# Retention's projections by Strassen's seven products for all heads first, results kept in DRAM, then the heads one by one

## The chip, the cores and the metric

The kernel runs on one core of one Trainium2 chip. Its time is device microseconds of that core; the figure of a kernel is the median of its runs. TensorE (PE in the profile) multiplies matrices into PSUM; VectorE (DVE) and ScalarE (ACT) work elementwise; GpSimd (POOL) works elementwise more slowly and issues DMAs, among them those that add into their target; SyncE (SP) issues the other DMAs.

## The reference

A decoder trunk of two layers on 512 tokens of 1024 features, in fp32. Each layer: half a SwiGLU FFN (2816 wide), a token mixer, half a FFN, a gated per-layer embedding. The mixer of layer 0 is retention with four heads, which is what the change touches:

```python
q, k, v, g = jnp.split(h @ w_in, ...)      # per head: 256, 256, 512, 512 columns
q = rotary(q, pos); k = rotary(k, pos) * DK ** -0.5
s = (q @ k.T) * decay                      # causal, per head
o = rmsnorm(s @ v, gn_w)                   # in chunks with a carried state; the kernel does it in one
y = silu(g) * o
h = h + y @ w_out
```

## The kernel before

Everything is kept transposed, features on partitions and the 512 tokens along the row. An fp32 value is split into a high part (a rounding to fp32r, made on ACT) and a low part (value minus high, DVE); a product is three matmuls, high x high, high x low, low x high (`mm3`, L330 to L332; `v_part` for values, L727 to L729; `product`, L515, for Strassen's). TensorE's instructions run in the order in which the code writes them; the other engines' order is made by a planner that places instructions as their inputs and tiles come free.

`Weights` holds a plan: the order in which weight tiles of 128 x 1024 are taken. `take` loads two tiles ahead (SP's queue), splits the tile on ACT and `W.low` (L85, L86; `W.low` is DVE, in the retention POOL) and has three buffers, `w8`. A `Pair` is Strassen's unit: two blocks of 128 output columns by two halves of the input features. Its two diagonal quarters get high and low parts in a `w8` tile: by ACT and DVE if the pair is marked `direct`, else by `negated` (L131 to L133): high on ACT, minus the raw value on ACT, then a DMA from POOL that adds the raw value into it. Four sums of quarters are made and split (`emit_sums_now`, L165), up to two pairs ahead. The FFNs take most pairs so: `start`, `one`, `two` begin pair m + 1 (three products) before `three` ends pair m (four products), with merges of PSUM banks between (L569 to L589); a pair is seven products of 12 matmuls of 256 columns. For this the norm makes seven forms of the activations per pair of feature blocks (`Norm.quarters`), where a plain projection needs only the high and low parts (`Norm.halves`).

The retention (L737 on) goes head by head, in plain projections `proj`, 24 matmuls of 512 columns for a block of 128 output columns: two query and two key blocks, `rotate`, the values (96 matmuls), the scores of the four key blocks with their decay and split (L819, `uhi`, `ulo`), then the previous head's output blocks or gate blocks, the products of scores and values (48 matmuls), gates, the scale of the head (`head_scale`, L773; `on_rows` with four transposes, L481, and a copy, L781) and the four outputs on DVE (L865, L869, L321). The output projections of the last two heads are summed in PSUM (`OutBoth`), and each finished block of h goes through the next norm's `quarters`.

The forgetting layer's values take weights by the adding DMA too (L133, `w<-in_fox_v`).

## Time and profile before

| what | value |
|---|---|
| median of three runs (lowest, highest) | 2148.61 us (2147.91, 2148.78) |
| profiled execution: time, span | 2147.82 us, 2145.9 us |
| TensorE busy, of the span | 2121.2 us, 99% |
| DVE, ACT, POOL busy | 1465.0, 1207.4, 355.9 us |
| retention, 348.6 to 752.6 us | 404.0 us |
| DVE, ACT, POOL busy in it | 183.2, 158.1, 143.4 us |
| granted TensorE clock | 0.998 |

How to read it: a TensorE that is busy throughout says only that matmuls follow each other; how long a stage takes is read from the number and width of its matmuls and the time between them. A row of a window gives its length, then busy time and number of instructions for each engine, the granted clock, the mean share in which the core's 16 DMA engines are busy, and GB/s. A row of a group ends in busy time, mean duration in ns, and the idle time just before with what ended it.

### The profile page before, as it was taken

The page shows a single profiled execution, that of the slowest core. Times are in us where ns is not written, and L with a number is a line of the kernel's source. Part 1 is how long each engine was busy: PE and PEld are TensorE (multiplying, and loading weights), DVE is VectorE, ACT ScalarE, POOL GpSimd, SP SyncE. Part 2 cuts the span into 40 slices and gives each one's busy share as a digit, 9 for nine tenths or more (in the row PEclk, how much of TensorE's full clock was granted, in tenths as well). Part 3 has the DMA queues.
Part 4 walks back from the last instruction along what each step waited for, and adds up shares of the span by engine and source line. Part 5 has one row for each costly group of instructions (what it writes and reads, how often), then busy time and mean ns, then how long its engine had stood idle before and what let it go on. Part 6 is the DMA issues. An engine that isn't in the chain of part 4 may idle for free.

```text
span 2145.9 us, 34373 instructions
## 1 busy us (share of the span) xinstructions
PE 2121.2 (99%) x13537; PEld 1917.5 (89%) x13537; DVE 1465.0 (68%) x2682; ACT 1207.4 (56%) x2036; POOL 355.9 (17%) x275
## 2 busy tenths in 40 slices
PE   9999999999999999999999999999999999999998
PEld 9899998888888898989989999998788799999987
DVE  8786876262533687868768787776675687877775
ACT  8474653333333664736557565555786775655655
POOL 0010100344444110201001011010234200100100
PEclk9999999999999999999999999999999999999999
DMA  6475652222222244746426466564522234655631
GB/s 192 119 177 134 161 150 93 88 94 79 89 79 89 91 124 131 181 124 174 130 94 153 125 169 155 142 148 122 144 84 93 80 99 125 171 153 142 158 108 40
DMA packets 92642, 268.39 MB, mean 125 GB/s; under 512 B 9392, under 2 KB 12976, under 8 KB 92480
## 3 DMA queue, kind: packets, MB, share of 16 engines
q1 hardware_dynamic: 63328, 209.78, 29.6%
q0 software_dynamic: 27920, 55.32, 15.7%
q8 instruction: 106, 1.74, 0.3%
q10 hardware_dynamic: 1232, 1.09, 0.2%
q14 instruction: 56, 0.46, 0.1%
HBM read 264.02 MB, written 2.13 MB: 124 GB/s over the span
## 4 chain that ended last, share of the span: by engine, by line
PE 84%; DVE 7%; ACT 5%; DMA 2%; issue 1%; SPq 0%; ACTq 0%; DVEq 0%
PE bank L515 35%; PE bank L330 13%; PE bank L332 13%; PE bank L331 13%; PE bank L550 3%; PE bank L728 2%; PE bank L727 2%; PE bank L729 2%; ACT p L1037 1%; DVE w L86 1%; DMA wraw<-in_ffn_w_in 1%; ACT p L1039 1%; DVE tlo L321 1%; ACT w L85 1%; DVE acc L454 1%
## 5 line engine op out<-in xcount | busy, mean ns | idle before, releaser
L85 ACT CAST w<-wraw 128x1024 fp32r<-128x1024 f32 (+1 forms) x234 | 238.5, 1022 | 420.1 <-PE bank L332 256.6
L330 PE MATMUL bank<-unit_a,w 128*128 128x512 f32 x736 | 287.9, 391 | 0.3 <-DVE tmp L1071 0.3
L331 PE MATMUL bank<-unit_a,w 128*128 128x512 f32 x736 | 286.6, 389 | 0.8 <-DVE unit_a L321 0.8
L332 PE MATMUL bank<-unit_a,w 128*128 128x512 f32 x736 | 286.6, 389 | 0.7 <-DVE w L86 0.7
L85 ACT CAST s<-sums 128x512 fp32r<-128x512 f32 x316 | 185.4, 618 | 149.7 <-PE bank L515 74.6
L330 PE MATMUL bank<-unit_d,w 128*128 128x512 f32 (+1 forms) x712 | 267.6, 376 | 1.0 <-DVE unit_b L324 0.6
L331 PE MATMUL bank<-unit_d,w 128*128 128x512 f32 (+1 forms) x712 | 266.8, 375 | 0.7 <-DVE unit_d L321 0.7
L332 PE MATMUL bank<-unit_d,w 128*128 128x512 f32 (+1 forms) x712 | 266.6, 374 | 0.0
L86 DVE TENSOR_TENSOR s<-sums,s 128x512 fp32r<-128x512 f32 x316 | 208.6, 686 | 60.9 <-ACT s L85 60.1
L86 POOL TENSOR_TENSOR w<-wraw,w 128x1024 fp32r<-128x1024 f32 x74 | 177.2, 2396 | 298.2 <-ACT w L85 293.3
L86 DVE TENSOR_TENSOR w<-wraw,w 128x1024 fp32r<-128x1024 f32 (+1 forms) x160 | 186.4, 1166 | 25.8 <-ACT w L85 25.7
L515 PE MATMUL bank<-unit_b,s 128*128 128x256 f32 x872 | 183.1, 276 | 0.0
L515 PE MATMUL bank<-unit_d,s 128*128 128x256 f32 x1140 | 178.3, 276 | 0.0
L133 POOL DMA_DIRECT2D a<-in_ffn_w_in x80 | 70.7, 884 | 630.0 <-ACT a L132 481.3
L515 PE MATMUL bank<-unit_a,s 128*128 128x256 f32 x1224 | 170.0, 276 | 0.0
L613 DVE SCALAR_TENSOR_TENSOR tmp<-bank,rows 128x512 f32<-128x512 f32 x96 | 66.2, 690 | 150.0 <-PE bank L332 149.9
L332 PEld LDWEIGHTS bank<-unit_a,w 128*128 128x128 f32 x736 | 138.2, 188 | 29.9 <-DVE w L86 1.1
L330 PEld LDWEIGHTS bank<-unit_a,w 128*128 128x128 f32 x736 | 138.2, 188 | 29.3 <-DVE tmp L1071 0.5
L331 PEld LDWEIGHTS bank<-unit_a,w 128*128 128x128 f32 x736 | 138.2, 188 | 29.2 <-DVE unit_a L321 1.2
L330 PEld LDWEIGHTS bank<-unit_d,w 128*128 128x128 f32 x712 | 133.8, 188 | 25.6 <-PE bank L1008 0.9
L331 PEld LDWEIGHTS bank<-unit_d,w 128*128 128x128 f32 x712 | 133.8, 188 | 24.4 <-DVE unit_d L321 1.0
L332 PEld LDWEIGHTS bank<-unit_d,w 128*128 128x128 f32 x712 | 133.7, 188 | 24.1
(295 smaller groups left out, 4758.7 us busy)
## 6 DMA issues: line engine op xcount, KB each, us to landing
wraw<-in_ffn_w_in SPq DMA_DIRECT2D x174, 512.0 KB, 4.4
wraw<-in_ffn_w_out SPq DMA_DIRECT2D x64, 512.0 KB, 4.4
w<-in_ffn_w_in POOLq DMA_DIRECT2D x57, 512.0 KB, 5.7
a<-in_ffn_w_in POOLq DMA_DIRECT2D x79, 256.0 KB, 6.2
wraw<-in_ffn_w_out SPq DMA_DIRECT2D x32, 384.0 KB, 3.7
wraw<-in_ret_qk SPq DMA_DIRECT2D x16, 512.0 KB, 3.5
wraw<-in_ret_v SPq DMA_DIRECT2D x16, 512.0 KB, 3.6
wraw<-in_ret_g SPq DMA_DIRECT2D x16, 512.0 KB, 3.5
```

The lines of the kernel that those rows point to most:

```text
L85: self.nc.scalar.copy(hi, raw)
L86: self.low.tensor_tensor(out=lo, in0=raw, in1=hi.bitcast(F32), op=ALU.subtract)
L133: self.nc.gpsimd.dma_start(out=lo, in_=src, accum_op=ALU.add)
L330: nc.tensor.matmul(out, wh, xh, start=first, stop=False)
L331: nc.tensor.matmul(out, wh, xl, start=False, stop=False)
L332: nc.tensor.matmul(out, wl, xh, start=False, stop=last)
L515: add = lambda w, x, start, stop: nc.tensor.matmul(out, w, x, start=start, stop=stop, skip_group_check=True)
L550: nc.tensor.matmul(o[:, HALVES[t]], x[:, ks], y, start=k == t == q == 0, stop=k == KB - 1 and q == 2, skip_group_check=True,)
L613: nc.vector.scalar_tensor_tensor(out=t1, in0=o, scalar=-0.5, in1=n.r, op0=ALU.mult, op1=ALU.mult)
L727: nc.tensor.matmul(os[t], xh, wh[:, js], start=k == 0, stop=False)
L728: nc.tensor.matmul(os[t], xh, wl[:, js], start=False, stop=False)
L729: nc.tensor.matmul(os[t], xl, wh[:, js], start=False, stop=k == KB - 1)
```

## The change

Strassen's pair code moves from the FFN into a class with `begin`, `rest` and `join` that hold the same operations. All four heads' queries and keys (eight pairs) and the gates of heads 1 to 3 (six pairs) are computed by it, so the norm ahead of the retention now makes the seven forms (with the corner `b12` in the tiles `ud`). The stage's order on TensorE is: values of head 1; pairs q1, k1; values of head 2; q2, k2, q3; values of head 3; k3, q0, k0; values of head 0; the six gate pairs. A pair's first three products stand ahead of the last four of the pair before it, across a values stage too. Rotated queries and keys of heads 1 to 3, all values and the gates of heads 1 to 3 (after SiLU) are written to DRAM by POOL's DMAs, 256 KB each; head 0's queries and keys stay on the chip, and its gates are computed later by plain products. The pairs 0 and 1 are `direct`, the others are not.

Then the heads run one by one. Each loads its queries, keys, values and gates from DRAM (SP's queue) and splits them again; scores and products follow each other, heads 1 to 3 with nothing between; output blocks of earlier heads stand elsewhere. The products loop over key blocks first, so that a head's four banks end together, and the sum of squares is on DVE, no longer on POOL. `W.low` stays DVE throughout; the output weights of heads 0 and 1 come by the adding DMA. Tile pools `ua` and `ud` change places in the FFNs behind. The weights' layout on the host follows.

```diff
+RET_V = {1: 2, 4: 3, 7: 0}
...
+    ret_order = [(x, hd) for hd in (1, 2, 3, 0) for x in "qk"] + [(x, hd) for hd in (1, 2, 3) for x in "01"]
...
-    ret_qk = [[a["ret_qk"][c] for c in (2 * h, 2 * h + 1, 8 + 2 * h, 9 + 2 * h)] for h in range(RH)]
     ret_v = [[a["ret_v"][h][:, c * 1024 : (c + 1) * 1024] for c in range(4)] for h in range(RH)]
-    ret_g = [[a["ret_g"][4 * h + c] for c in range(4)] for h in range(RH)]
+    ret_g = [[a["ret_g"][c] for c in range(4)]]
+    at = {"q": 0, "k": 4, "0": 8, "1": 9}
+    ret_pairs = []
+    for kind, hd in ret_order:
+        i = at[kind] + (hd if kind in "qk" else 2 * (hd - 1))
+        ret_pairs.append(Pair(4, a["ret_p"][i, 0], a["ret_p"][i, 1]))
+    ret_pairs[0].direct = ret_pairs[1].direct = True
...
     plan_ffn(0)
-    for h in range(RH - 1):
-        W.plan += ret_qk[h] + ret_v[h]
-        if h > 0:
-            W.plan += ret_o[h - 1]
-        W.plan += ret_g[h]
-    W.plan += ret_qk[RH - 1] + ret_v[RH - 1] + ret_g[RH - 1][0:2] + ret_o[RH - 2][0:1] + ret_g[RH - 1][2:4]
-    W.plan += ret_o[RH - 2][1:2]
+    W.plan += ret_v[1] + ret_pairs[0:1]
+    for i in range(len(ret_pairs)):
+        W.plan += ret_pairs[i + 1 : i + 2]
+        if i in RET_V:
+            W.plan += ret_v[RET_V[i]]
+    W.plan += ret_g[0] + ret_o[0] + ret_o[1] + ret_o[2][0:2]
     W.plan += [ret_o[i][c] for i, c in ((RH - 1, 0), (RH - 2, 2), (RH - 1, 1), (RH - 1, 2), (RH - 2, 3), (RH - 1, 3))]
...
+    def proj_forms(src, n):
+
+        wh, wl = W.take(src)
+        o = bank()
+        for t, half in enumerate(HALVES):
+            for k in range(KB):
+                ks = slice(k * P, (k + 1) * P)
+                xh, xl = n.forms[k // 2][f"b{1 + k % 2}{1 + t}"]
+                for q, (w, x) in enumerate(((wh, xh), (wh, xl), (wl, xh))):
+                    nc.tensor.matmul(
+                        o[:, half], w[:, ks], x, start=k == t == q == 0, stop=k == KB - 1 and q == 2,
+                        skip_group_check=True,
+                    )
+        return [o]
+
...
+    class Strassen:
+
+
+        def __init__(self, n):
+            self.n, self.live = n, {}
+
...
+        def rest(self, pair):
+            c0, c1 = HALVES
+            forms = self.n.forms
+            g, u, cc = self.live[id(pair)]
+            product(u[:, c0], pair.t[1], 0, forms, "t4")
+            product(g[:, c1], pair.s[3], 0, forms, "b22")
+            product(u[:, c1], pair.s[2], 0, forms, "t3")
+            product(g[:, c0], pair.x, 0, forms, "b21")
+
+        def join(self, pair):
...
+            return g, u
+
...
                     mm3(o, wh[:, js], wl[:, js], *act[k], k == k0, k == k1 - 1)
             for m, o in zip(ms, os):
+                if m == KB - 1 and c == len(chunks) - 1 and nxt.early and nxt.extra:
+                    nxt.corner(range(KB // 2))
...
         last = plain(done - 1, {10: scaled})
-        start(done)
-        one(done)
-        two(done)
+        by7.begin(ins[done])
         gated(done - 1, *last, True)
...
+    def open_retention():
+
+        stack = ExitStack()
+        hold = stack.enter_context(tc.tile_pool(name="hold", bufs=1, reuse_waits="tile"))
+        sums = ExitStack()
+        W.open(4, sums.enter_context(tc.tile_pool(name="rsum", bufs=2, reuse_waits="tile")))
+        return stack, hold, sums
+
+    def retention(n, nxt, pools):
+        stack, hold, sums = pools
...
+        qd, kd = kept[0:4], kept[4:8]
+        vd = [kept[8 + 2 * i : 10 + 2 * i] for i in range(RH)]
+        gd = [kept[16 + 2 * i : 18 + 2 * i] for i in range(RH)]
+        slot = lambda i: stat.tile([P, S], F32, name="acc") if i else hold.tile([P, S], F32, name="slot")
+        cs, sn = slot(1), slot(0)
+        nc.sync.dma_start(out=cs, in_=a["rot"][0])
...
+        new = lambda: unit(ud)
+
+        def rotate(x1, x2, to):
+
+            out = []
+            for s, (p, q, op) in enumerate(((cs, sn, ALU.add), (sn, cs, ALU.subtract))):
+                t1, t2 = temp(), temp()
+                nc.vector.tensor_tensor(out=t1, in0=x1, in1=p, op=ALU.mult)
+                nc.vector.tensor_tensor(out=t2, in0=x2, in1=q, op=ALU.mult)
+                nc.vector.tensor_tensor(out=t1, in0=t1, in1=t2, op=op)
+                if to is None:
+                    out.append((new(), new()))
+                    split(t1, *out[-1])
+                else:
+                    nc.gpsimd.dma_start(out=to[:, s, :], in_=t1)
+            return out
+
+        def gates(x1, x2, to):
+            for s, (x, sign) in enumerate(((x1, 1.0), (x2, -1.0))):
+                t1 = temp()
+                nc.vector.tensor_tensor(out=t1, in0=x, in1=n.r, op=ALU.mult)
+                nc.scalar.activation(t1, t1, AF.Silu, scale=sign)
+                nc.gpsimd.dma_start(out=to[:, s, :], in_=t1)
+
+        def values(hd, to):
...
+            for t in range(NT):
+                t1 = temp()
+                nc.scalar.copy(t1, os[t])
+                nc.gpsimd.dma_start(out=to[t // 2][:, t % 2, :], in_=t1)
+
+        def fetched(src, pool=ud):
+
+            out = []
+            for s in range(2):
+                hi, lo = new(), unit(pool)
+                raw = lo.bitcast(F32)
+                nc.sync.dma_start(out=raw, in_=src[:, s, :])
+                nc.scalar.copy(hi, raw)
+                nc.vector.tensor_tensor(out=lo, in0=raw, in1=hi.bitcast(F32), op=ALU.subtract)
+                out.append((hi, lo))
+            return out
+
+        by7, got = Strassen(n), {}
+
+        def finished(i):
+            kind, hd = ret_order[i]
+            x = by7.join(ret_pairs[i])
+            if kind in "qk":
+                got[kind, hd] = rotate(*x, None if hd == 0 else {"q": qd, "k": kd}[kind][hd])
+            else:
+                gates(*x, gd[hd][int(kind)])
+
+        W.begin(())
+        values(1, vd[1])
+        by7.begin(ret_pairs[0])
+        n.columns()
+        nc.vector.tensor_scalar(out=epsc, in0=n.v, scalar1=EPS, scalar2=None, op0=ALU.mult)
+        nc.vector.tensor_tensor(out=rk2, in0=n.c, in1=n.c, op=ALU.mult)
+        for i in range(len(ret_pairs)):
+            if i + 1 < len(ret_pairs):
+                by7.begin(ret_pairs[i + 1])
+            by7.rest(ret_pairs[i])
+            finished(i)
+            if i == 0:
+                n.rows()
+            if i in RET_V:
+                values(RET_V[i], vd[RET_V[i]])
+        sums.close()
+
+        pool = stack.enter_context(tc.tile_pool(name="ret", bufs=1, reuse_waits="tile"))
+
+        def loaded(hd):
+            where = ud if hd else ua
+            values = lambda: fetched(vd[hd][0], where) + fetched(vd[hd][1], where)
+            return values() if hd == 0 else (fetched(qd[hd]), fetched(kd[hd]), values())
+
+        def scores(hd, q, kk):
+            dk = slot(hd % 2)
+            nc.sync.dma_start(out=dk, in_=a["decay"][hd])
+            u = []
...
+            return u
+
+        def attended(v, u):
+            os = [bank() for _ in range(4)]
+            for j in range(NT):
+                for d, o in enumerate(os):
+                    ds_ = slice(d * P, (d + 1) * P)
+                    mm3(o[:, j * P : S], v[j][0][:, ds_], v[j][1][:, ds_], *u[j], j == 0, j == NT - 1)
...
+        def gate(c):
+            (g,) = proj_forms(ret_g[0][c], n)
+            t1 = temp()
+            nc.vector.tensor_tensor(out=t1, in0=g, in1=n.r, op=ALU.mult)
+            s_ = pool.tile([P, S], F32, name="sg", bufs=8)
+            nc.scalar.activation(s_, t1, AF.Silu)
+            return s_
+
+        def kept_gates(hd):
+            out = []
+            for x in gd[hd]:
+                for s in range(2):
+                    s_ = pool.tile([P, S], F32, name="sg", bufs=8)
+                    nc.sync.dma_start(out=s_, in_=x[:, s, :])
+                    out.append(s_)
+            return out
+
...
+        out_w, y = {}, [([], []) for _ in range(RH)]
+        W.by_dma |= {id(x) for hd in (0, 1) for x in ret_o[hd]}
+        v = loaded(0)
+        u = scores(0, got["q", 0], got["k", 0])
+        sg = [gate(0)]
+        os, acc = attended(v, u)
+        q, kk, v = loaded(1)
+        sg.append(gate(1))
+        rn = head_scale(acc)
+        sg.append(gate(2))
+        rn = on_rows(rn)
+        sg.append(gate(3))
+        outputs(0, os, sg, rn, y[0])
+        u = scores(1, q, kk)
+        os, acc = attended(v, u)
+        q, kk, v = loaded(2)
+        sg = kept_gates(1)
+        out_blocks(0, y[0], range(0, 3))
+        rn = head_scale(acc)
+        out_blocks(0, y[0], range(3, 5))
+        rn = on_rows(rn)
+        outputs(1, os, sg, rn, y[1])
+        out_blocks(0, y[0], range(5, 8))
+        u = scores(2, q, kk)
+        os, acc = attended(v, u)
+        q, kk, v = loaded(3)
+        sg = kept_gates(2)
+        out_blocks(1, y[1], range(0, 3))
+        rn = head_scale(acc)
+        out_blocks(1, y[1], range(3, 5))
+        rn = on_rows(rn)
+        outputs(2, os, sg, rn, y[2])
+        out_blocks(1, y[1], range(5, 6))
+        u = scores(3, q, kk)
+        os, acc = attended(v, u)
+        sg = kept_gates(3)
+        out_blocks(1, y[1], range(6, 7))
+        both = OutBoth([(ret_o[2], *y[2]), (ret_o[3], *y[3])], nxt)
+        both.first((0, 1))
+        rn = head_scale(acc)
+        out_blocks(1, y[1], range(7, 8))
+        rn = on_rows(rn)
+        both.first((2, 3))
+        outputs(3, os, sg, rn, y[3])
+        stack.close()
         stack = open_ffn(1)
         first_pair(1)
...
 
-    bca, bcd, bdc = ((ub, 8), (uc, 4), (ua, 16)), ((ub, 8), (uc, 4), (ud, 16)), ((ub, 8), (ud, 16), (uc, 4))
-    where = (bca, ((ua, 16),), bca, ((ua, 16),), bdc, ((ud, 16),), bcd, ((ud, 16),))
+    bca, bcd, bac = ((ub, 8), (uc, 4), (ua, 16)), ((ub, 8), (uc, 4), (ud, 16)), ((ub, 8), (ua, 16), (uc, 4))
+    where = (bca, bca, bcd, ((ud, 16),), bac, ((ua, 16),), bca, ((ua, 16),))
     norms = [Norm(nw(i), *where[i]) for i in range(8)] + [Norm(fw)]
-    norms[4].extra = norms[6].extra = ua
-    norms[2].extra = ud
-    norms[4].early = True
+    norms[1].extra = norms[4].extra = norms[6].extra = ud
+    norms[2].extra = ua
+    norms[1].early = norms[4].early = True
...
-    stack = ffn_ple(1, 0, norms[2], norms[3], norms[4], stack, ud, 1)
-    ffn(2, norms[4], norms[5], stack, ua)
+    pools = []
+    ffn(0, norms[0], norms[1], stack, ud, lambda: pools.append(open_retention()))
+    stack = retention(norms[1], norms[2], pools[0])
+    stack = ffn_ple(1, 0, norms[2], norms[3], norms[4], stack, ua, 1)
+    ffn(2, norms[4], norms[5], stack, ud)
     stack = forgetting(norms[5], norms[6])
-    ffn_ple(3, 1, norms[6], norms[7], norms[8], stack, ua, 2)
+    ffn_ple(3, 1, norms[6], norms[7], norms[8], stack, ud, 2)
 
```

More of the change, by code (lines that the diff above doesn't have):

```diff
@@ L530, in ffn @@
         c0, c1 = HALVES
-        live, act = {}, {}
+        act, by7 = {}, Strassen(n)
         def plain(m, between={}):
@@ L646, in ffn @@
                 if begun < k1:
-                    start(begun)
-                    one(begun)
-                    two(begun)
+                    by7.begin(ins[begun])
                     begun += 1
-                three(m)
-                finish(m)
+                by7.rest(ins[m])
+                gated(m, *by7.join(ins[m]), False)
             done = k1
             if begun < NF:
-                start(begun)
-                one(begun)
-                two(begun)
+                by7.begin(ins[begun])
                 begun += 1
@@ L877, in retention @@
-            W.low = nc.vector
-            both.first((2, 3))
-            outputs()
+                    out=t1[:, :w], in0=s[:, :w], scalar=rk2[:, j : j + 1], in1=dk[:, :w],
+                    op0=ALU.mult, op1=ALU.mult,
+                )
+                hi = pool.tile([P, w], F32R, name=f"uhi{j}", bufs=2)
+                lo = pool.tile([P, w], F32R, name=f"ulo{j}", bufs=2)
+                split(t1[:, :w], hi, lo)
+                u.append((hi, lo))
+            return u
+        def attended(v, u):
+            os = [bank() for _ in range(4)]
+            for j in range(NT):
+                for d, o in enumerate(os):
+                    ds_ = slice(d * P, (d + 1) * P)
+                    mm3(o[:, j * P : S], v[j][0][:, ds_], v[j][1][:, ds_], *u[j], j == 0, j == NT - 1)
+            acc = None
+            for d in range(4):
+                sq = temp()
+                nc.scalar.activation(sq, os[d], AF.Square)
+                if acc is None:
+                    acc = sq
+                else:
+                    nc.vector.tensor_tensor(out=acc, in0=acc, in1=sq, op=ALU.add)
+            return os, halved(acc)
@@ new lines, in head_scale, with on_rows @@
+        def head_scale(parts):
+            total = over_tokens(parts)
+            v, t, rn = (pool.tile([P, NT], F32, name=x) for x in ("rv", "rt", "rn"))
+            nc.vector.scalar_tensor_tensor(
+                out=v, in0=total, scalar=1.0 / S, in1=epsc, op0=ALU.mult, op1=ALU.add
+            )
+            rsqrt(rn, v, t)
+            return rn
+        def on_rows(rn):
+            rows = pool.tile([P, S], F32, name="rnrows")
+            nc.scalar.copy(rows, spread(rn))
+            return rows
@@ new lines, in outputs @@
+        def outputs(hd, os, sg, rn, y):
+            for d in range(4):
+                t1 = temp()
+                nc.vector.scalar_tensor_tensor(
+                    out=t1, in0=os[d], scalar=gnw[:, 4 * hd + d : 4 * hd + d + 1], in1=rn,
+                    op0=ALU.mult, op1=ALU.mult,
+                )
+                nc.vector.tensor_tensor(out=t1, in0=t1, in1=sg[d], op=ALU.mult)
+                hi, lo = unit(ua), unit(ua)
+                split(t1, hi, lo)
+                y[0].append(hi)
+                y[1].append(lo)
@@ new lines, in out_blocks @@
+        def out_blocks(hd, y, ms):
+            for m in ms:
+                if m % 2 == 0:
+                    out_w[hd] = W.take(ret_o[hd][m // 2])
+                wh, wl = out_w[hd]
+                o = bank()
+                for k in range(4):
+                    ks = slice((4 * (m % 2) + k) * P, (4 * (m % 2) + k + 1) * P)
+                    mm3(o, wh[:, ks], wl[:, ks], y[0][k], y[1][k], k == 0, k == 3)
+                nc.vector.tensor_tensor(out=h[m], in0=o, in1=h[m], op=ALU.add)
+        out_w, y = {}, [([], []) for _ in range(RH)]
@@ L1374, in _layout @@
         "ffn_w_out": np.stack([tiles(wo[i]) for i in range(4)]),
-        "ret_qk": c(tiles(rw[:, :2048])),
+        "ret_p": quarters(np.concatenate([tiles(rw[:, :2048]), tiles(rw[:, 4608:])]).reshape(14, 2, P, D).transpose(1, 0, 2, 3)),
         "ret_v": c(wide(rw[:, 2048:4096])),
-        "ret_g": c(tiles(rw[:, 4096:])),
+        "ret_g": c(tiles(rw[:, 4096:4608])),
         "ret_o": c(outp(ret_w_out[0])),
```

208 lines of the change are left out of this document (47 added, 161 removed).

## The prediction

> **What bounds the kernel now.** I read the page's first part, then the busy time by stage in windows, then TensorE's waits inside the retention.
>
> ```profile
> span 2145.9 us, 34373 instructions
> PE 2121.2 (99%) x13537; PEld 1917.5 (89%) x13537; DVE 1465.0 (68%) x2682; ACT 1207.4 (56%) x2036; POOL 355.9 (17%) x275
> ...
> core 0: us, PE busy (x) PEld busy (x) DVE busy (x) ACT busy (x) POOL busy (x), PEclk, DMA share, GB/s
> 112.10:188.80 76.70, 76.70 (x673) 76.70 (x672) 64.70 (x115) 55.58 (x97) 12.70 (x13) 1.00 0.74 181
> 305.00:348.60 43.60, 43.60 (x195) 36.10 (x194) 27.89 (x38) 17.14 (x23) 0.00 (x0) 1.00 0.36 117
> 451.00:472.70 21.70, 21.70 (x97) 17.99 (x96) 7.85 (x9) 6.95 (x9) 10.94 (x5) 1.00 0.30 103
> 348.60:752.60 404.00, 402.20 (x1885) 337.43 (x1884) 183.22 (x279) 158.06 (x221) 143.44 (x66) 1.00 0.26 86
> ```
>
> The four windows are eight Strassen pairs of the first FFN, that FFN's last output blocks, one head's values, and the whole retention. The reader is to see that TensorE has work in all of them, at a granted clock of 1.00, while VectorE (DVE) in the retention is busy 183 of 404 us. Waits in the retention are almost nothing:
>
> ```profile
> engine line waited for: us in total, times, longest us
> PE bank L331 <- DVE unit_d L321: 0.7, 1, 0.7
> PE bank L332 <- DVE w L86: 0.7, 1, 0.7
> PE bank L330 <- DVE tmp L833: 0.4, 1, 0.4
> ```
>
> That is 1.8 us in all. So TensorE's matmul time sets the end. The change can gain only by fewer matmul columns, and it loses whatever new waits it brings.
>
> **What is removed.** The values window holds 96 matmuls of 512 columns in 21.70 us, so 0.226 us each, and a plain pair of column blocks (48 of them) takes 10.85 us. The Strassen window holds 672 matmuls of 256 columns in 76.70 us, 0.114 us each, so a Strassen pair (84) takes 9.59 us. Fourteen pairs change form: 14 x (10.85 - 9.59) = 17.7 us less. Values, scores, head 0's gates and output blocks keep their matmuls. The old waits go too, 1.8 us.
>
> **Added work at nothing, and its cover.** The last blocks of FFN 0 now make Strassen's forms for the next norm: per block some 0.8 us more of DVE, and 1.7 us of corners once, 8 us in all. The second window has DVE at 27.89 of 43.60 us, so it stays below TensorE; without that cover it would cost up to 8 us at the retention's start. The first values stage (21.7 us) stands before the first pair and uses the last block's forms last.
>
> ```profile
> 142.33 0.43 DVE L588 TENSOR_TENSOR bank<-bank,tmp 128x256 f32<-128x256 f32 x1
> 142.66 0.68 DVE L165 TENSOR_TENSOR sums<-sums,wraw 128x512 f32<-128x512 f32 x1
> 143.26 0.69 DVE L165 TENSOR_TENSOR sums<-wraw 128x512 f32<-128x512 f32 x1
> 143.87 0.42 DVE L589 TENSOR_TENSOR bank<-bank,tmp 128x256 f32<-128x256 f32 x1
> ```
>
> Back to back a 512-column DVE operation costs 0.60 us and a 256-column one 0.33 us. A query or key pair needs 4 sums, 4 low parts, 4 merges and 6 rotation steps: 14 x 0.60 + 4 x 0.33 = 9.7 us against TensorE's 9.59. Runs of three such pairs lie between values stages in which DVE has four weight splits at most, so 0.3 us of lag is caught up; I take nothing. Late next would be the sums of the following pair.
>
> **The first pair after a values stage.** Weight tiles share three buffers. While values stage V runs, the begun pair holds one until its t4 product behind V, so V's four tiles turn over in two, and the next pair's tile gets the buffer that V's third tile frees, 16.3 us into V. This pair is not "direct": its low part is made by ScalarE (ACT) twice and an accumulating DMA from POOL.
>
> ```profile
> 117.90 1.05 ACT L131 CAST w<-wraw 128x1024 fp32r<-128x1024 f32 x1
> 118.85 1.06 ACT L132 ACTIVATE w<-wraw 128x1024 fp32r<-128x1024 f32 x1
> ...
> 120.21 1.08 POOL L133 DMA_DIRECT2D w<-in_ffn_w_in  x1 [16.11 <-ACT w L132]
> ...
> w<-in_ffn_w_in POOLq DMA_DIRECT2D x57, 512.0 KB, 5.7
> s<-in_ffn_w_in POOLq DMA_DIRECT2D x1, 512.0 KB, 9.5
> ...
> PE bank L728 <- DMA w<-in_fox_v: 1.1, 1, 1.1
> ```
>
> From the first copy to the issue it is 2.3 us, from issue to landing 5.7: ready at 16.3 + 2.3 + 5.7 = 24.3 us. TensorE wants the low part after eight matmuls, at 21.7 + 0.9 = 22.6. That is a wait of 1.7 us, three times (pairs 3, 6 and 9): 5.1 us. The last row shows this kind of wait in the forgetting layer's values now. Bounds: 0 if the buffer is had one tile earlier, 5.5 each (16.5) if every landing takes the longest 9.5. I take 5.1, as the loads are light in a values stage (DMA share 0.30).
>
> **The heads one by one.** Before, projections stood between a head's scores and the products that use them; now these follow directly, with an output block or gate beside them only ahead of the scores. DVE first has the previous head's outputs to do:
>
> ```profile
> 712.45 0.60 PE L481 MATMUL bank<-ident,rn 128*128 128x128 f32 x4
> 713.75 1.28 ACT L835 ACT_TABLE_LOAD   x1
> 715.05 0.63 ACT L835 ACTIVATE sg<-tmp 128x512 f32<-128x512 f32 x1
> 715.59 0.57 ACT L781 COPY rnrows<-bank 128x512 f32<-128x512 f32 x1
> 716.19 1.41 DVE L865 SCALAR_TENSOR_TENSOR tmp<-bank,small,rnrows 128x512 f32<-128x512 f32 x2 [1.19 <-ACT rnrows L781]
> ...
> 723.35 1.22 DVE L86 TENSOR_TENSOR w<-wraw,w 128x1024 fp32r<-128x1024 f32 x1
> 724.49 0.68 DVE L321 TENSOR_TENSOR unit_d<-tmp,unit_d 128x512 fp32r<-128x512 f32 x1
> ...
> L819 DVE SCALAR_TENSOR_TENSOR tmp<-bank,rk,decay 128x512 f32<-128x512 f32 x4 | 3.0, 751 | 0.7 <-PE bank L332 0.5
> L320 ACT CAST uhi<-tmp 128x512 fp32r<-128x512 f32 x4 | 2.5, 622 | 2.4 <-DVE tmp L819 2.4
> L321 DVE TENSOR_TENSOR ulo<-tmp,uhi 128x512 fp32r<-128x512 f32 x4 | 6.4, 1602 | 0.0
> L321 DVE TENSOR_TENSOR vlo<-bank,unit_c 128x512 fp32r<-128x512 f32 x16 | 10.9, 692 | 51.6 <-ACT unit_c L320 51.6
> ```
>
> Four outputs take 716.19 to 725.17, less the 1.14 us of a weight split between: 7.8 us. The chain from a score to its low part is 0.75 + 0.62 + 0.69 = 2.1 us (I take the values' 0.69 for the low part; the score's own row, 1.60, was taken while POOL split weights, which the change ends, and would add 0.9 to each wait). Let R be the time when the head's rows are copied, about 0.8 us after TensorE's transposes free it. TensorE then has until the product: head 3, one output block (12 x 0.226 = 2.7) and scores (7,680 columns, 3.4), free at R + 5.3; DVE has 7.8 of outputs, 0.6 of one addition and the chain, R + 10.5: wait 5.2 us. Head 2 has three blocks: R + 10.8 against 7.8 + 1.8 + 2.1 = R + 11.7, wait 0.9. Head 1 has a gate of 5.4, done at R + 4.6, and scores to R + 8.1; its fourth output needs that gate's product, table load and SiLU (0.69 + 1.28 + 0.63, R + 7.2) and then three steps of 0.6 to 0.7, R + 9.1, with the score's low part 0.5 behind: R + 9.6, wait 1.5. Head 0 has a gate between scores and product: nothing there; but its squares end together now, 4.3 us of chain beside 1.6 of splits against a gate of 5.4: 0.5.
>
> ```profile
> 705.93 0.95 PE L344 MATMUL bank<-ones_r,tmp 128*128 128x2 f32 x8
> 706.91 0.16 DVE L773 SCALAR_TENSOR_TENSOR rv<-bank,epsc 128x4 f32<-128x4 f32 x1
> ...
> 709.94 0.17 DVE L490 SCALAR_TENSOR_TENSOR rn<-rt,rn 128x4 f32<-128x4 f32 x1
> ```
>
> The last head's scale takes 3.4 us from TensorE's sums to the transposes, with one block of 2.7 beside it: 0.7. Sum: 0.5 + 1.5 + 0.9 + 5.2 + 0.7 = 8.8 us. Bounds: 1.2 (three chains that the later scores nearly cover, if the planner puts scores ahead of outputs on DVE) and 19 (two weight splits of 1.22 inside each stretch and no overlap).
>
> **Traffic through DRAM.** 40 writes and 40 reads of 256 KB are added.
>
> ```profile
> q1 hardware_dynamic: 63328, 209.78, 29.6%
> q0 software_dynamic: 27920, 55.32, 15.7%
> ```
>
> These rows give 3.0 and 6.1 us of all 16 engines per MB. A Strassen pair uses 0.74 x 9.59 = 7.1 us of them now; two writes add 1.6 by the first price and 3.2 by the second: 8.7 to 10.3 of 9.59. I take the middle, below the brim, and no wait. On POOL's queue a write that waits for a rotation holds up the accumulation of a later pair; on SP's, a fetch that waits for a free tile holds up weight loads two tiles (10 us) ahead; both have that much room.
>
> **Sum.** -17.7 - 1.8 + 5.1 + 8.8 = -5.6 us. The profiled execution took 2147.8 us on the clock of the runs for a span of 2145.9; the median is 2148.6. So span 2140.3, time 2143.0 us. A measurement can tell 0.2%, 4.3 us, from no change.
>
> **Rivals.**
> The waits are hidden (the planner orders DVE well, the buffer comes early): -17.7 - 1.8 + 0 + 1.2, about 2130. For it: DVE has 220 us free in the retention. Against: no matmul is left between scores and product. Chance 0.23.
>
> DMA engines fill: with the upper price from the pairs on, landings go to 9.5 us, so the waits after values cost 16.5, and the five last pairs, with no values stage behind, lose 0.7 each, 3.5: -19.5 + 16.5 + 8.8 + 3.5 = +9.3, 2157.9. It decides once two writes cost over 2.5 us. For it: 0.74 is busy already; against: loads are spread by three values stages. Chance 0.16.
>
> Seven temporaries: a query or key pair takes seven (copy, two small, four in the rotation), two of them held until a write lands, so the next pair's copy can wait. Priced at 0 to 2 us for each of eight pairs, the middle gives +8: 2151. Chance 0.13.
>
> The clock falls: nine matmuls at the start, out of idleness, took twice the 0.226 us.
>
> ```profile
> 1.59 4.21 PE L315 MATMUL bank<-tmp,ones_r 128*128 128x512 f32 x9 [1.59 <-DVE tmp L313]
> ```
>
> If the 5.2 us wait of head 3 brings that state back for such a stretch, half of some 3.6 us is lost: +1.8, 2144.8. Chance 0.06. [...]
>
> **How the numbers follow.** The forecast keeps 0.42, its own range 2138 to 2148. Faster by over 0.2% (below 2144.3): 0.27 of that, 0.23 of hidden waits, 0.03 of the clock: 0.53. Slower by over 0.2% (above 2152.9): 0.14 of the full engines and 0.04 of the temporaries, 0.18. The rest, 0.29, is within. The range 2132 to 2156 cuts the ends of the hidden waits and of the full engines.
>
> **What would show it.** The Strassen pairs of the retention at 0.114 us a matmul; a wait of the next pair for its accumulating DMA behind three values stages, 1 to 3 us; a wait for a score's low part (ulo) of some 5 us at head 3 and less at 1 and 2; granted clock 1.00; DMA share of the query and key pairs near 0.9. The forecast is wrong if copies into temporaries or landings hold TensorE between pairs, or if no wait stands between scores and product.

## The result and the profile after

The changed kernel takes 2174.35 us (median of 5 runs, 2167.42 to 2174.87) beside 2148.61 us before (5 runs, 2147.91 to 2149.36): 1.011 times as long, interval 1.0099 to 1.0121. The forecast was 2143.0 with a range up to 2156; it is missed by 31 us, and on the wrong side. The profiled run took the median itself.

Windows of the kernel after (length; busy time and instructions of PE, PEld, DVE, ACT, POOL; granted clock; DMA share; GB/s):

```profile
349.60:779.40 429.80, 404.58 (x2486) 367.63 (x2485) 283.38 (x493) 228.84 (x369) 55.14 (x74) 0.96 0.59 165
418.70:424.10 5.40, 1.23 (x11) 0.99 (x9) 0.00 (x0) 2.65 (x4) 2.58 (x4) 0.89 1.06 267
424.10:427.50 3.40, 3.40 (x16) 3.40 (x17) 0.00 (x0) 0.00 (x0) 0.00 (x0) 0.50 0.91 205
431.00:436.00 5.00, 5.00 (x45) 5.00 (x43) 2.84 (x6) 4.00 (x8) 1.09 (x1) 1.00 0.05 9
563.00:590.00 27.00, 27.00 (x229) 27.00 (x228) 19.63 (x35) 16.98 (x30) 7.23 (x10) 1.00 0.90 240
```

The retention lasts 429.8 us instead of 404.0: +25.8. The profiled spans differ by 26.7 (2172.6 and 2145.9); the kernel after loses the other 1.0 us in its first 12 us. The reader is to see three things. The row from 418.70 is a wait of TensorE, with the DMA engines full, at a share of 1.06. The row from 424.10, right behind, has TensorE busy throughout, but at a granted clock of 0.50, 16 matmuls in 3.40 us where the row from 431.00 has 45 in 5.00. And the gate pairs (563 to 590), with the DMA engines at 0.90, have no wait. TensorE's waits in the retention (line, what it waited for, us in total, times, longest):

```profile
PE bank L336 <- ACT uhi L326: 13.5, 2, 9.8
PE bank L537 <- DMA w<-in_ret_p: 10.8, 3, 4.2
```

Five waits make nearly all of it: three for the adding DMA behind the values stages (4.3, 4.2 and 2.8 us by the gaps between matmuls, at 424.05, 482.72 and 539.70), and two for a score's high part, at head 1 (10.1) and head 3 (3.9). The first one in the chain of waits, and the DMAs that SP and POOL send at that time:

```profile
413.54 2.33 issue
...
415.88 8.12 DMA w<-in_ret_p
...
424.05 3.14 PE bank L537 x13
```

```profile
415.61 0.33 SPq L79 DMA_DIRECT2D wraw<-in_ret_p  x1
```

```profile
415.88 1.12 POOL L134 DMA_DIRECT2D w<-in_ret_p  x1 [13.57 <-ACT w L133]
417.81 1.90 POOL L821 DMA_DIRECT2D kept<-tmp  x3 [0.81 <-ACT tmp L820]
```

The buffer was freed at 413.54 and the adding DMA sent 2.33 us later, as worked out; but it landed after 8.12 us, not 5.7 (7.98 and 6.57 behind the other two stages). A load of 512 KB from SP starts 0.27 us ahead of it, and the values' writes follow 2 us behind it. Now head 1, in the chain and on ACT and DVE:

```profile
636.95 8.45 DMA unit_d<-kept
...
645.50 0.62 ACT unit_d L830
...
647.21 0.79 PE bank L336
```

```profile
633.62 0.69 DVE L925 TENSOR_TENSOR tmp<-bank,rows 128x512 f32<-128x512 f32 x1 [5.49 <-PE bank L522]
634.23 1.40 DVE L942 SCALAR_TENSOR_TENSOR tmp<-bank,small,rnrows 128x512 f32<-128x512 f32 x2
```

```profile
645.50 0.62 ACT L830 CAST unit_d<-unit_d 128x512 fp32r<-128x512 f32 x1 [4.59 <-DMA unit_d<-kept]
646.03 0.61 ACT L326 CAST unit_a<-tmp 128x512 fp32r<-128x512 f32 x1
646.55 0.61 ACT L326 CAST uhi<-tmp 128x512 fp32r<-128x512 f32 x1
```

Two queues are held here. DVE stands 5.49 us before the product of head 0's last gate, which TensorE gives it only then, and the outputs begin behind that. ACT stands 4.59 us before the cast of a fetched tile of the next head, whose transfer took 8.45 us; the score's high part (`uhi`) is two places behind. Head 3's wait is the chain that the forecast told, DVE's outputs first:

```profile
708.26 1.41 DVE tmp L942 x2
...
716.40 1.58 DVE tmp L881 x3
717.98 0.61 DVE ulo L327
718.63 0.80 PE bank L337
```

Last, one matmul of the sums' tiles (`s`) by its duration (least, median, greatest ns), after and before:

```profile
L537 PE MATMUL bank<-unit_a,s x80: 283/283/283, 563.5 to 589.9; 128*128 128x256 f32 x80
```

```profile
L515 PE MATMUL bank<-unit_a,s x220: 276/276/276, 119.8 to 177.8; 128*128 128x256 f32 x110
```

They overlap, so the durations are not their spacing, but the 7 ns are also in the spacing of their starts: 0.120 us in the retention, 0.113 in the first FFN.

### The profile page after: what moved, and what is told of

The parts are those of the page before. It is cut to its first block, busy times and chain, and to the rows that moved or that the text cites. A ratio compares the mean times of both kernels' runs of the same rounds, so it can differ in the third digit from the quotient of the medians.

```text
span 2172.6 us, 36216 instructions
## 1 busy us (share of the span) xinstructions
PE 2124.4 (98%) x14137; PEld 1948.7 (90%) x14137; DVE 1569.7 (72%) x2913; ACT 1283.7 (59%) x2202; POOL 268.5 (12%) x284
## 4 chain that ended last, share of the span: by engine, by line
PE 83%; DVE 7%; ACT 4%; DMA 3%; issue 2%; SPq 0%; DVEq 0%; ACTq 0%; POOLq 0%
PE bank L537 42%; PE bank L336 11%; PE bank L337 11%; PE bank L338 11%; PE bank L614 3%; PE bank L816 1%; PE bank L817 1%; PE bank L815 1%; DMA w<-in_ret_p 1%; ACT p L1164 1%; PE bank L522 1%; DVE w L87 1%; DMA wraw<-in_ffn_w_in 1%; ACT p L1166 1%; DVE tlo L327 1%
## 5 line engine op out<-in xcount | busy, mean ns | idle before, releaser
L87 DVE TENSOR_TENSOR s<-sums,s 128x512 fp32r<-128x512 f32 x372 | 246.2, 686 | 125.7 <-ACT s L86 124.8
L537 PE MATMUL bank<-unit_a,s 128*128 128x256 f32 x2202 | 328.3, 279 | 0.0
L537 PEld LDWEIGHTS bank<-unit_a,s 128*128 128x128 f32 x2202 | 290.4, 190 | 0.0
L337 PE MATMUL bank<-unit_d,w 128*128 128x512 f32 x656 | 255.5, 389 | 0.8 <-DVE unit_d L327 0.8
L336 PE MATMUL bank<-unit_d,w 128*128 128x512 f32 x656 | 255.7, 390 | 0.3 <-DVE tmp L1198 0.3
L338 PE MATMUL bank<-unit_d,w 128*128 128x512 f32 x656 | 255.3, 389 | 0.0
L537 PE MATMUL bank<-unit_b,s 128*128 128x256 f32 x1040 | 223.5, 279 | 0.0
L336 PE MATMUL bank<-unit_a,w 128*128 128x512 f32 (+1 forms) x536 | 199.9, 373 | 1.0 <-DVE unit_b L330 0.6
L337 PE MATMUL bank<-unit_a,w 128*128 128x512 f32 (+1 forms) x536 | 198.6, 371 | 0.0
L338 PE MATMUL bank<-unit_a,w 128*128 128x512 f32 (+1 forms) x536 | 198.4, 370 | 0.0
L537 PEld LDWEIGHTS bank<-unit_b,s 128*128 128x128 f32 x1040 | 168.0, 191 | 0.0
L537 PE MATMUL bank<-unit_b,w 128*128 128x256 f32 x837 | 154.6, 283 | 10.8 <-DMA w<-in_ret_p 10.8
L537 PE MATMUL bank<-unit_a,w 128*128 128x256 f32 x978 | 150.6, 279 | 1.5 <-ACT tmp L565 1.5
L537 PE MATMUL bank<-unit_c,s 128*128 128x256 f32 x682 | 152.1, 281 | 0.0
L337 PEld LDWEIGHTS bank<-unit_d,w 128*128 128x128 f32 x656 | 123.2, 188 | 26.3 <-DVE unit_d L327 1.2
```

The source lines that it names most:

```text
L87: self.low.tensor_tensor(out=lo, in0=raw, in1=hi.bitcast(F32), op=ALU.subtract)
L336: nc.tensor.matmul(out, wh, xh, start=first, stop=False)
L337: nc.tensor.matmul(out, wh, xl, start=False, stop=False)
L338: nc.tensor.matmul(out, wl, xh, start=False, stop=last)
L537: add = lambda w, x, start, stop: nc.tensor.matmul(out, w, x, start=start, stop=stop, skip_group_check=True)
```

## The experiments

All are edits of the kernel after. "Before" in the batches took 2148.6 to 2149.5 us.

**Pairs 3, 6 and 9 direct.** The low part is made by DVE, without the adding DMA.

```diff
-    ret_pairs[0].direct = ret_pairs[1].direct = True
+    for i in (0, 1, 3, 6, 9):
+        ret_pairs[i].direct = True
```

> Pairs 3, 6 and 9, the first behind a values stage, are marked direct, so that their low parts come from DVE and not from an adding DMA. Theory A (the buffer comes late and the adding DMA behind it lands late; the granted clock then falls for some 7 us): the three waits of 4.2, 4.2 and 2.8 us go below 1 us each, and with them three clock falls of about 2.8 us: 10.8 + 8.4 = 19 us less, some 2155 us. Rival B (the DMA engines are full at that place, so raw tiles and sums are late whichever way the low part is made): at least half of the waits stay, 2164 us or more.

Measured 2155.15 us, 1.0028 of before (1.0016 to 1.004). The three waits are gone. They cost 19.2 us, though their length is 10.8 to 11.3.

**The clock apart from the waits.** Matmuls without use fill the three waits; the pairs start no earlier.

```diff
+    for i, k in ((3, 34), (6, 33), (9, 22)):
+        ret_pairs[i].warm = k
...
             g, u = bank(), bank()
+            for _ in range(getattr(pair, "warm", 0)):
+                nc.tensor.matmul(g[:, c0], ones_r, forms[0]["b11"][0], start=True, stop=True, skip_group_check=True)
```

> 34, 33 and 22 matmuls of 256 columns whose result is thrown away stand on TensorE ahead of pairs 3, 6 and 9, 4.1, 4.0 and 2.6 us, so that they fill the wait. Theory A (a wait of 3 to 4 us makes the granted clock fall to half for the next 5 to 7 us): the granted clock stays 1.00 there, each wait turns into matmuls of the same length, and about 8 us are saved, 2166 us. Rival B (the slow matmuls behind the wait come from the DMA traffic of that place, not from the wait): the clock falls all the same and the time stays at 2174 us or grows by up to 1.

Measured 2166.47, 1.0081 (1.0066 to 1.0096). The windows behind the three places:

```profile
419.50:426.50 7.00, 7.00 (x62) 7.00 (x61) 1.02 (x2) 1.95 (x4) 1.70 (x2) 1.00 1.00 272
475.00:482.00 7.00, 6.93 (x59) 6.73 (x58) 0.69 (x1) 2.20 (x4) 1.69 (x2) 1.00 1.01 263
532.00:539.00 7.00, 6.68 (x57) 6.47 (x56) 2.15 (x4) 2.19 (x5) 1.58 (x2) 1.00 1.05 280
```

The clock stays at 1.00 and 7.9 us come back by the medians, 2.6 for each fall. So the 19.2 us are 11.3 of waiting and 7.9 of a clock halved behind it. The granted clock of the kernel after says about the same. These are the 7 us behind each of its five waits, the three of the pairs, then heads 1 and 3:

```profile
424.05:431.05 7.00, 7.00 (x37) 7.00 (x38) 1.12 (x2) 1.40 (x3) 0.00 (x0) 0.59 0.74 174
482.72:489.72 7.00, 7.00 (x40) 7.00 (x41) 1.29 (x3) 1.48 (x3) 0.00 (x0) 0.64 0.75 181
539.70:546.70 7.00, 7.00 (x36) 7.00 (x37) 1.12 (x2) 1.22 (x3) 0.51 (x1) 0.56 0.91 242
647.21:654.21 7.00, 6.98 (x23) 5.57 (x24) 4.31 (x10) 2.24 (x5) 0.00 (x0) 0.68 0.81 278
717.77:724.77 7.00, 6.93 (x20) 5.46 (x21) 3.21 (x7) 0.97 (x3) 0.00 (x0) 0.60 0.25 75
```

What is missing to 1.00, times 7 us, is 2.9, 2.5, 3.1, 2.2 and 2.8 us: 8.5 behind the pairs' waits and 13.5 in all.

**How long a wait must be.** The same with 14, 20 and 8 matmuls.

> 14, 20 and 8 matmuls of 256 columns without use stand ahead of pairs 3, 6 and 9, so that TensorE idles about 2.5, 2.0 and 3.2 us there and not 4.1, 4.3 and 4.1; the pairs start no later than before. It asks from what length of a wait the clock falls. Theory A (below some 2.7 us it doesn't, near 3 us it is chance, as a wait of 2.78 us was followed by a clock of 0.5 and one of 3.06 us in another kernel by 1.0): clock 1.00 behind the first two, the third open; 2168 us. Rival B (it falls after any wait over 2 us): 0.5 behind all three, and 2174 as without the edit.

Measured 2167.87, 1.0088 (1.0073 to 1.0103). The waits left were 1.4, 2.2 and 3.6 us. Behind the first the clock stayed at 1.00, behind the other two it fell (0.60 and 0.62 over the 3.40 us from 478.00 and 535.90). The time is theory A's, but its mechanism failed: 2.2 us were enough. Rival B fails too: in the run that moves the load (below) the clock stayed at 1.00 behind a wait of the same 2.2 us, and in the run with another order of splits behind one of 3.06. So length alone doesn't decide.

The granted clock in the traces tells more. In the kernel after it falls to 0.50 six times ahead of the fall at the kernel's end. From the first fall, at 422.96, to the last rise, at 1573.25, every change comes a whole multiple of 3.41 us behind the one before, so at marks 3.41 us apart, and the six low stretches last 6.83, 6.83, 6.83, 10.24, 6.83 and 3.41 us. Here is the time behind the first wait of this run; then its wait of 2.2 us, from one mark to the next, and the stretch behind it; then the wait of 3.06 us of the run with another order of splits, in two stretches that meet at 537.70, where I estimate a mark (the clock doesn't change there):

```profile
421.60:425.00 3.40, 3.40 (x28) 3.40 (x29) 0.55 (x1) 1.11 (x2) 0.23 (x1) 1.00 0.78 241
475.27:478.68 3.41, 1.41 (x12) 1.20 (x12) 0.00 (x0) 0.00 (x0) 1.49 (x2) 1.00 1.05 320
478.68:482.09 3.41, 3.41 (x19) 3.41 (x18) 0.22 (x1) 0.86 (x2) 0.00 (x0) 0.50 1.04 208
534.29:537.70 3.41, 1.53 (x11) 1.25 (x9) 0.00 (x0) 3.00 (x4) 1.63 (x4) 1.00 1.07 205
537.70:541.11 3.41, 2.40 (x20) 2.40 (x21) 0.00 (x0) 0.18 (x1) 1.25 (x2) 1.00 0.96 342
```

By the trace's matmul ends TensorE was idle for 2.00 of the 3.41 us in the first case, for 1.88 and 1.01 in the second. In the retention of the kernel after, the stretches between two marks that end at its five falls were idle for 90, 67, 56, 100 and 70% (1.92 us in the third, 0.04 more than the 1.88 behind which the other run's clock stayed), and no other stretch there at a clock of 1.00 for more than 19%. The idle share alone doesn't decide either. The sixth fall, in the forgetting layer, came behind a stretch idle for 1.35 us, 40%, and none came behind one of 1.50 in the first FFN, 44%:

```profile
1566.43:1569.84 3.41, 2.06 (x9) 1.38 (x9) 3.29 (x7) 3.34 (x9) 2.98 (x2) 1.00 0.02 4
1569.84:1573.25 3.41, 3.41 (x11) 2.93 (x11) 3.41 (x18) 1.84 (x5) 2.28 (x1) 0.50 0.44 153
67.97:71.38 3.41, 1.91 (x17) 1.72 (x16) 3.03 (x8) 2.60 (x6) 0.85 (x1) 1.00 0.65 184
71.38:74.79 3.41, 3.41 (x31) 3.41 (x31) 2.72 (x5) 1.99 (x3) 0.00 (x0) 1.00 0.77 177
```

So where a wait lies between the marks may decide with its length; no run here moves a wait against them. By length alone, the clock fell behind waits of 2.2 and 2.8 us, not behind another of 2.2 nor one of 3.06, and behind the five of 3.6 to 10.1 in this run's pairs and the kernel after.

**Why the adding DMA is late: the queue?** The values' writes go by SP.

```diff
-                nc.gpsimd.dma_start(out=to[t // 2][:, t % 2, :], in_=t1)
+                nc.sync.dma_start(out=to[t // 2][:, t % 2, :], in_=t1)
```

> The values' writes (four of 256 KB per head) go from POOL's queue to SP's; nothing else. It asks why the adding DMA of pairs 3, 6 and 9 takes 6.6 to 8.1 us, not 5.7. Theory A (it shares the 16 DMA engines with the writes that are sent 2 to 6 us behind it): the transfer takes 7 to 8 us as before, the three waits stay at 3 to 4 us, 2172 us give or take 3. Rival B (it is the queue of POOL that serves them together): the transfer falls to 5.7 us, the waits to 2 us each, so 6 us less and some of the clock: 2164.

Measured 2176.67, 1.0121 (1.0108 to 1.0134). The transfer became no shorter, so serving writes and adding DMA by one queue isn't the cause. The three took 9.05, 9.04 and 8.18 us, and the waits grew to 14.4 us in all, more than theory A had. The first:

```profile
414.46 9.05 DMA w<-in_ret_p
```

**The writes?** Those of heads 2, 3 and 0 are left out.

```diff
-                nc.gpsimd.dma_start(out=to[t // 2][:, t % 2, :], in_=t1)
+                if hd == 1:
+                    nc.gpsimd.dma_start(out=to[t // 2][:, t % 2, :], in_=t1)
...
-            values = lambda: fetched(vd[hd][0], where) + fetched(vd[hd][1], where)
+            values = lambda: fetched(vd[1][0], where) + fetched(vd[1][1], where)
```

> Left out: the values of heads 2, 3 and 0 are computed and copied but not written to DRAM, and these heads fetch head 1's values in their place (the same number and size of fetches). So the adding DMA of pairs 3, 6 and 9 runs without the four writes beside it. Theory A (the transfer takes 6.6 to 8.1 us because it shares the DMA engines with those writes): the transfer takes 5.7 us or less, the three waits fall from 4.3, 4.2 and 2.8 us to about 1.7 each, the size forecast, and the clock no longer falls behind them; 2174 - 6 - 8 = 2160 us. Rival B (the transfer has that length in this stage anyway): waits of 3 to 4 us stay, 2172.

Measured 2174.14, 1.012 (1.0103 to 1.0137): nothing. The first transfer:

```profile
414.47 7.99 DMA w<-in_ret_p
```

The other two took 6.12 and 8.22; with the writes the three were 8.12, 7.98 and 6.57. My theory A, which the run before seemed to bear out, falls. What stayed in both is the load from SP 0.27 us ahead: ACT's negated copy ends, and with it both the adding DMA and the load into the tile just read may start.

**The load?** It goes behind the adding DMA in POOL's queue.

```diff
     def load(self, src, behind=None):
...
+            with self.tc.issue_after(behind.ins):
+                self.nc.gpsimd.dma_start(out=raw[:, : src.shape[1]], in_=src)
...
+    for i in (3, 6, 9):
+        ret_pairs[i + 2].late = ret_pairs[i]
```

> The load of 512 KB that SP sends 0.27 us ahead of the adding DMA of pairs 3, 6 and 9 (the second tile of the pair two further on, into the raw tile that ScalarE's negated copy frees) goes behind the adding DMA in POOL's queue; all else stands. Theory C, new after the run without writes (the adding DMA takes 6.1 to 8.2 us and not 5.5 because a load of 512 KB starts beside it at the same moment; the 26 adding DMAs with a load that starts at most 2 us before or 1 us behind took 7.7 us in the median, the 58 others 5.6): the transfer takes 5.5 to 6 us, the waits fall to 1.5 to 2.2 us each, the clock falls behind one or none, 2174 - 6 - 5 = 2163 us. Rival (the length belongs to this stage, whatever runs beside): 6.5 to 8 us, 2172.

Measured 2161.73, 1.0055 (1.0038 to 1.0072). Chain of waits, TensorE's waits, and the window behind the first:

```profile
415.58 5.67 DMA w<-in_ret_p
```

```profile
PE bank L544 <- DMA w<-in_ret_p: 5.2, 3, 2.0
```

```profile
421.30:424.70 3.40, 3.40 (x28) 3.40 (x29) 0.54 (x1) 1.11 (x2) 1.73 (x2) 1.00 1.01 365
```

5.67, 5.40 and 5.96 us to landing, gaps of 1.9, 1.6 and 2.2, no fall of the clock, though the DMA engines are as full as before, at a share of 1.01 behind the first. Theory C holds, and with the load moved the forecast's 5.7 and its 1.7 a pair come out to a few tenths. The edit moves the load to the adding DMA's own queue and also makes it start later, 0.87 us behind the adding DMA in the first of the three, and it doesn't part the two. One row of the kernel after speaks for the queue: an adding DMA of the forgetting layer, at 1546.41, took 8.4 us with loads that SP sent 0.5 and 0.9 us behind it.

**Load moved and no writes.**

> Left out, as in the run without writes: the values of heads 2, 3 and 0 are not written, these heads fetch head 1's. With it the load behind the adding DMA. Theory C: 5.4 to 5.7 us, waits of 1.5 to 2 us, 2162 us, no more than 2 us from the run with the writes. Rival D (load and writes each fill what the other leaves): here 5.5 us, but with the writes 7.

Measured 2161.79, 1.0058 (1.0043 to 1.0073), with 4.6 us of waits for the three: as with the writes. The load alone makes the difference; rival D is out.

**The order of the fetched tiles' splits** (heads 2 and 3, that is, during the scores of heads 1 and 2).

```diff
+        def behind_scores(hd):
+            with tc.issue_after(self_last[0].ins), tc.issue_after(self_last[1].ins):
+                return loaded(hd)
...
-        q, kk, v = loaded(2)
+        q, kk, v = behind_scores(2)
```

> ACT's and DVE's splits of the next head's fetched tiles are queued behind the splits of this head's last score (heads 1 and 2). Theory A (at head 1 ACT stands before the cast of the next head's fetched query, whose DMA takes 8.4 us, while the score's cast is queued behind): the wait of 10.1 us falls to 7.5, where DVE's late outputs let the score's chain end (642.6 + 2.1 against TensorE free at 637.2); 2172 us. Rival B (the forecast's chain alone, without the late outputs): it falls to 1.5, 2164 us with the clock. Rival C (ACT's order is not the cause): it stays at 10.

Measured 2168.89, 1.0092 (1.0073 to 1.0111).

```profile
PE bank L336 <- ACT uhi L326: 10.6, 2, 6.7
```

Head 1's wait falls from 9.8 to 6.7 by this view: ACT's cast was a third of it, and DVE's chain behind the gate is the rest, as theory A had it. The time fell by 5.5 us; in the profiled run the clock also stayed up behind the third pair's wait (the 3.06 us above).

**Work between scores and products.**

```diff
-        sg.append(gate(3))
-        outputs(0, os, sg, rn, y[0])
         u = scores(1, q, kk)
+        sg.append(gate(3))
+        outputs(0, os, sg, rn, y[0])
         os, acc = attended(v, u)
...
         u = scores(3, q, kk)
-        os, acc = attended(v, u)
         sg = kept_gates(3)
         out_blocks(1, y[1], range(6, 7))
+        os, acc = attended(v, u)
```

> One cause alone, the waits for a score's parts at heads 1 and 3: a piece of work that stood elsewhere is put between scores and products, head 0's fourth gate (5.4 us) at head 1, the last two output blocks of head 1 that come before the joint output (2.7 us for the one moved) at head 3. Theory A (no matmul stands between scores and products; the two waits of 10.1 and 3.9 us follow from it, and the clock falls after them): the wait at head 1 goes, that at head 3 falls to 1 or 2 us, the clock stays at 1.00 behind head 1; 2174 - 10.1 - 2.5 - 2.8 - 1 = 2157 us. Rival B (at head 1 ScalarE's cast of a fetched tile, late by a slow transfer, holds the queue whatever TensorE does): the wait only shrinks by the 5.4 us of the gate, 2166. Rival C: the time is as without the edit, since the work moved leaves a gap where it stood, 2172.

(The expectation's "two output blocks" is the one block 6 of head 1; block 7 stays.) Measured 2161.55, 1.0057 (1.0044 to 1.007):

```profile
PE bank L336 <- ACT uhi L326: 3.1, 3, 1.7
```

13.5 us became 3.1, the clock stays up (1.00 over the 3.40 us from 638.00 and from 676.00), 12.8 us come back of the 17 expected: a smaller wait came up at head 2, and the three waits behind the values were longer in this run, 12.2 us. Nearer A than B in mechanism, between them in time. Rival C is out.

**The tiles' addresses.** In the compiled program, whose addresses no trace shows, the sums' tiles lie 256 bytes (modulo 512) behind the activations that they multiply, 192 in the FFNs; the retention's pool ahead of them makes the difference. A tile without use of 448 bytes restores 192. (Of a pair's 84 matmuls 60 have such weights, not 72 as the expectation says.)

```diff
         epsc = hold.tile([P, NT], F32, name="epsc")
+        hold.tile([P, 112], F32, name="pad")
```

> A tile of 448 bytes that nothing uses is added to the pool that lies below the pairs' sums, so that the sums start at 224 bytes past a multiple of 512, as in the FFNs, and not at 288. Theory A (the place of the stationary operand against the moving one sets the matmul's time): matmuls whose weights are sums take 0.113 us in place of 0.120, 14 pairs x 72 such matmuls x 0.0065 = 6.5 us less, about 2168 us. Rival B (the DMA writes or the other engines' traffic slow TensorE in this stage): 0.120 stays and the time is 2174 us.

Measured 2169.64, 1.0099 (1.0082 to 1.0116), 4.7 us less. That interval overlaps the one of the kernel after, so the time alone doesn't show the gain; the duration of a matmul does:

```profile
L537 PE MATMUL bank<-unit_a,s x84: 276/276/276, 563.0 to 589.8; 128*128 128x256 f32 x84
```

Three more sizes, one run each:

> A tile of 64 bytes without use ahead of the sums' tiles: in the compiled program they lie 320 bytes (modulo 512) behind the activations that they multiply, 256 in the kernel after. Theory A (the two operands are slow together when their offset is a multiple of 256): 0.113 us a matmul of the sums' tiles. Rival B (192 alone is fast): 0.120.

> The tile has 128 bytes, the offset is 384. Theory A: 0.113. Rival B: 0.120.

> The tile has 256 bytes, the offset is 0. Theory A: 0.120, as without the tile. Rival C (any move of the tiles away from where they were does it): 0.113.

Offsets of 320, 384 and 0, in that order:

```profile
L537 PE MATMUL bank<-unit_a,s x69: 276/276/284, 564.4 to 586.0; 128*128 128x256 f32 x69
```

```profile
L537 PE MATMUL bank<-unit_a,s x75: 279/281/285, 563.1 to 588.1; 128*128 128x256 f32 x75
```

```profile
L537 PE MATMUL bank<-unit_a,s x75: 283/283/283, 563.3 to 589.8; 128*128 128x256 f32 x75
```

Medians of 276, 281 and 283 ns, a spacing of 0.114, 0.119 and 0.120 us; the single times were 2163.36, 2175.51 and 2170.89, and say little, since the waits differed too. Here 0 and 256 were slow and 192 and 320 fast, as A had it, but 384 was not fast. Rivals B and C are out, and A's rule is too simple. No run moves the activations alone, so whether the offset between the two or the weights' own place counts isn't shown, and why it counts stays open.

**All together.** Direct pairs, 448 bytes, work between scores and products:

> Three causes at once: pairs 3, 6 and 9 direct, the sums' tiles moved to 224 modulo 512 bytes, the two pieces of work between scores and products. Theory A (the causes are separate and add up): 18.8 us for the direct pairs and 4.5 for the tiles, as each measured alone, and 17 for the waits of the heads, off 2174: 2134 us, so faster than the kernel before by 0.7%. Rival B (they share one bound, the DMA engines, which takes back part of it): 2142 to 2150. Granted clock above 0.996 by A.

Measured 2141.62 (2137.63 to 2147.56), 0.9965 of before (0.9953 to 0.9977): 7.6 us faster than the kernel before, 32.7 faster than the one after, with a granted clock of 0.994 to 0.998. The sum of theory A, 2134, is missed by 8 us; rival B's range starts at 2142, so its time came nearer, but no run here shows that the causes share a bound. The longest waits in the retention that are left:

```profile
PE bank L337 <- ACT uhi L327: 2.4, 3, 0.9
PE bank L337 <- DVE tmp L927: 1.2, 1, 1.2
```

With the order of splits as a fourth:

> The same three with a fourth: the splits of the fetched tiles of the next head stand behind the split of the last score in the order of ScalarE and VectorE (alone it gave some 4 us). Theory A: with a gate between scores and products the order no longer matters; 2134 us, within 2 of the kernel without the fourth. Rival B: the cast that holds ScalarE's queue is still in the way, and the fourth edit brings 3 us more: 2131.

Measured 2141.0, 0.9963 (0.995 to 0.9976): no more, as A had it. Both are 7 to 8 us over A's sum. The moved work had given 4 us less than its forecast already when alone; the rest, of which the small waits above may be a part, is not split.

## Why the prediction was wrong, point by point

- **Fewer columns, -17.7.** Right in number of matmuls, wrong in one assumption: "0.114 us each" was taken from a stage whose tiles lie otherwise. 60 of a pair's 84 matmuls, 14 pairs, 7 ns each: +5.9 us by estimate (4.7 between medians in the run that moved the tiles). Head 0's gates, now 192 matmuls of 256 columns at that same slower pace, 0.120 us each, add 1.3.
- **The first pair behind a values stage, +5.1.** The mechanism, the freed buffer and the 2.3 us were right. "From issue to landing 5.7" failed: it was taken from the FFN, where a load from SP starts at most 2 us ahead of the adding DMA, or 1 us behind it, in only 8 of 57 cases. Here the same copy on ACT frees both, and 6.6 to 8.1 us made 10.8 of 5.1. The upper bound, 9.5 each, held. The profile before had a nearer row: the adding DMAs of the forgetting layer's values, each sent 0.27 us behind a load from SP.

```profile
w<-in_fox_v POOLq DMA_DIRECT2D x4, 512.0 KB, 7.2
```

With 7.2 in place of 5.7 the same working gives 3.2 us a pair, 9.6 in all.

- **The heads, +8.8.** Head 3: 5.2 forecast, 3.9 measured, by the chain told. Head 2: 0.9 forecast, 0.3 measured, for `ulo`. Head 0 and the last scale: 0.5 and 0.7 forecast, 0.2 and 0.3. Head 1 failed: 1.5 forecast, 10.1 measured. The step let DVE begin the outputs while the gate ran; in DVE's order the gate's product stands ahead of them. And no step asked what stands ahead of `uhi` on ACT: the cast of a fetch for the next head, that waits for a slow transfer. In all 14.3 us of waits in place of 8.8 (13.5 for `uhi` by the view, 0.8 in the three short ones).
- **The clock.** The rival "the clock falls" had the mechanism right and the size wrong: chance 0.06, one wait, 1.8 us. It was five waits, 2.2 to 3.1 us each, 13.5 in all. The rival reckoned with head 3's 5.2 us alone; here a wait of 2.8 us, and in the run with fewer matmuls in the waits one of 2.2, was enough. Neither fills the 3.41 us between two marks: the stretch with the wait of 2.2 us was idle for 59%, the one with 2.8 for 56%.
- **Sum.** -17.7 - 1.8 + 10.8 + 14.3 + 13.5 + 5.9 + 1.3 = +26.3; the retention grew by 25.8 in the profiled runs, the median by 25.7. The pairs' waits are 10.8 or 11.3 by the way of counting, so an agreement within half a microsecond is partly luck.
- **Right.** The work added at nothing cost nothing (the FFN ahead has no new wait). DMA share in the pairs near 0.9, 0.90 seen, without a wait in the gate pairs. The rival of the full engines had longer landings behind the values, and they came, but not by its cause: the values' writes changed nothing when left out, and the load did when moved. Its time, 2157.9, came nearest of all and is still 16 us short. No wait for temporaries of more than 0.2 us. "Waits are hidden" is out.

So the forecast's sign turned on waits that it sized too small and on the clock behind them, which it gave a chance of 0.06. With the three causes mended together the change gives 7.6 us of the 19.5 that its sum holds.

## What to carry to other kernels

Price a new wait at its length plus what the clock loses behind it: here some 2.7 us behind each of five waits of 2.8 to 10 us, so 25 us of waiting cost 38. Take a transfer's time from a row in which the same transfers start beside it: what frees its tile may free another's too. And for each new dependence read the queues of all the engines on its path, not only the operations in it: at head 1 two instructions that belonged to other heads decided.
